# Streamed weight tiles of 1024 columns instead of 512 in a decoder block with product-key experts

## The chip, the core and the metric

The kernel runs on one core of a Trainium2 chip. The metric is the device time of one execution in microseconds (us), over the runs given below. Its matrix engine is called TensorE (PE in the profile), its elementwise engine VectorE (DVE), its activation engine ScalarE (ACT), its general engine GpSimd (POOL); SyncE (SP) issues most transfers. Sixteen DMA engines move data between memory and the on-chip buffers, and PSUM banks take what TensorE computes.

## The reference

One sequence of 1024 tokens with 1024 features goes through a mixing half and an expert half. Cut to what matters:

```python
h = rmsnorm(x, norm_mix_w)
z = h @ w_in
zs, zq, zk, zv, zg = split(z)
ya = rwkv7_time_mix(token_shift(zs, mu), ...)
yb = diff_attention(zq, zk, zv, ...)
ga, gb = split(zg)
merged = sigmoid(ga) * (ya @ proj_a) + sigmoid(gb) * (yb @ proj_b)
x = x + merged @ w_out
hf = rmsnorm(x, norm_ffn_w)
q = hf @ w_q
s = einsum('thcd,hcnd->thcn', q, sub_keys)
ids, gates = top16_of_the_pair_sums(s)       # 8 heads x 16 experts for a token
act = gelu(einsum('ced,cd->ce', u_tab[ids], hf)) * gates
x = x + einsum('ce,ced->cd', act, v_tab[ids])
return rmsnorm(x, final_norm_w)
```

`u_tab` and `v_tab` have 16384 rows (experts) of 1024 numbers.

## The kernel before

**Products in three parts.** Every large float32 product is made of three faster ones. A matrix is split into `hi`, its rounding to the faster type (ScalarE, a copy), and `lo`, the rest (VectorE, a subtraction); `hi x hi`, `hi x lo` and `lo x hi` are added up in PSUM. `wsplit` (L147) loads a streamed weight tile of 128 x 512 as `wraw`, and makes `whi` and `wlo`. `wmul` (L156) takes two such tiles for one output tile of 128 features by 512 tokens: 8 steps of 128 columns, three matmuls each. There are four buffers for `wraw` and three each for `whi` and `wlo`.

**The mixing half.** It runs for tokens 0 to 511, then for 512 to 1023 (`mix`). Each group makes 42 tiles `z` from `w_in` by `wmul`, between them four recurrent heads (`rwkv`) and four attention heads (`attention`), then the merge with `proj`, then `w_out`. A recurrent head inverts small triangles in the tile `z16`, which starts as an identity: VectorE copies the constant `eye16` into it (L370). `pick` makes queries and keeps the best 16 of each half key; `choose` makes the indices and gates of 128 tokens, in tiles `ids` and `gate`.

**The experts, for tokens 0 to 511: gathers.** `peer` (L787) does 128 tokens at a time. For each of the 128 picks, GpSimd issues a DMA that gathers one row of `u` for each token into one of five `uv` buffers (L773), and VectorE multiplies it with `hb` and sums (L795). Then the same with rows of `v`, which VectorE multiplies by `act` and adds to `acc` (L802). That makes 1024 gathers of 512 KB in all. They begin while the second group is mixed, and go on beside the rest of the kernel.

**The experts, for tokens 512 to 1023: dense.** `gates` (L804) turns the indices into a table of gates for every expert and token, `gd_s`. `dense` (L844) then goes through all experts in 128 blocks of 128. For block e, `head` makes `ua`, the product of the block of `u` and the tokens (24 matmuls, weights by `wsplit`; the first 16 blocks are made earlier, by `ahead`, and read back). ScalarE applies gelu (`gw`), VectorE multiplies it with the gates (L865) and both split it into `ah` and `al`. The block of `v` comes in two halves `vraw` of 128 x 512 (six buffers), each split into `vh` and `vl`; the left half has four pairs of buffers, the right half three. Then eight output tiles add three matmuls each. Six of them stay in PSUM banks for the whole loop (`yk`). The two others (`yr`) take a bank every second block, for two blocks at a time (`rest`), and VectorE adds that bank to `accd` (L885). `ua` and `yr` share two banks.

**What sets the order.** Tiles come from pools with a number of buffers for each name, and a new tile waits until a buffer is free. A scheduler in the build puts the instructions of every engine, and each engine's transfers, in one fixed order, from the dependencies, the buffers and its own idea of what an operation costs. On the chip each engine keeps that order, and waits where something is not there yet. So the products of the gathers stand at fixed places between the other instructions of VectorE.

Of the kernel before, what the change touches and what calls it, by code (L numbers as in the profile page):

```python
# [8 lines left out]
F32 = mybir.dt.float32  # L9
F32R = mybir.dt.float32r  # L10
BF = mybir.dt.bfloat16
I32 = mybir.dt.int32
U32 = mybir.dt.uint32
AF = mybir.ActivationFunctionType
OP = mybir.AluOpType
# [16 lines left out]
NB = 5  # L32
NW = 3
NRAW = 4
NVR = 6
# [7 lines left out]
NV = (8, 6)  # L43
# [3 lines left out]
def body(ctx: ExitStack, tc: tile.TileContext, ins, out, dbg=None):  # L47
# [49 lines left out]
    def const(name, shape, dt=F32):  # L97
        t = kp.tile(shape, dt, name=name)
        nc.sync.dma_start(t, ins[name])
        return t  # L100
# [10 lines left out]
    eye16 = const("eye16", [64, 16, 16])  # L111
    blk = const("blk", [P, P])
    rmask = const("rmask", [P, 512])
    dist = const("dist", [P, T])
    lam4 = const("lam4", [64, 4])
    eye_row = const("eye_row", [P, P])
# [30 lines left out]
    def wsplit(src):  # L147
        raw = wp.tile([P, 512], F32, name="wraw", bufs=NRAW)
        nc.sync.dma_start(raw, src)
        hi = wp.tile([P, 512], F32R, name="whi", bufs=NW)  # L150
        lo = wp.tile([P, 512], F32R, name="wlo", bufs=NW)
        nc.scalar.activation(hi, raw, AF.Copy)  # L152
        nc.vector.tensor_tensor(lo, raw, hi.bitcast(F32), op=OP.subtract)  # L153
        return hi, lo

    def wmul(o, src, xh, xl, n=8, step=1):  # L156

        w = []  # L160
        for k0 in range(0, n, step):
            ks = range(k0, k0 + step)
            for k in ks:
                if k % 4 == 0:
                    w.append(wsplit(src[k // 4]))
                hi = w[-1][0][:, (k % 4) * P:(k % 4 + 1) * P]
                nc.tensor.matmul(o, hi, xh(k), start=(k == 0), stop=False)  # L167
                nc.tensor.matmul(o, hi, xl(k), start=False, stop=False)  # L168
            for k in ks:
                lo = w[k // 4][1][:, (k % 4) * P:(k % 4 + 1) * P]  # L170
                nc.tensor.matmul(o, lo, xh(k), start=False, stop=(k == n - 1))  # L171
# [71 lines left out]
    def mix(gi, t0, W):  # L243
# [13 lines left out]
        def zt(ct):  # L257
            b = zbank("z")[:, :W]
            wmul(b, ins["w_in"][ct], lambda k: hh_[:, k, :W], lambda k: hl_[:, k, :W])
            return b  # L260
# [18 lines left out]
        def rwkv(h, kz, rz, vz):  # L279
# [90 lines left out]
            nc.vector.tensor_copy(z[nn], eye16[nn])  # L370
# [244 lines left out]
        for d in range(8):  # L615
            m = []
            for i in range(2):
                sgm = at("sgm")[:, :W]
                nc.sync.dma_start(sgm, ins["g_s"][gi, 8 * i + d, :, :W])
                b = zbank("pj")[:, :W]  # L620
                wmul(b, ins["proj"][d, i:i + 1], lambda k: yh[4 * i + k], lambda k: yl[4 * i + k], 4)
                t = mg[d // 2][:, d % 2 * 512:d % 2 * 512 + W] if i == 0 else sgm
                nc.vector.tensor_tensor(t, sgm, b, op=OP.mult)
                m.append(t)
            nc.vector.tensor_tensor(m[0], m[0], m[1], op=OP.add)
            show("mrg", m[0], (d, slice(None), slice(t0, t0 + W)))
            mcat.append(m[0])
# [11 lines left out]
        for k in range(8):  # L639
            w = [wsplit(ins["w_out"][k, i]) for i in range(2)]  # L640
            for a in range(TT):
                o = slice(a * P, (a + 1) * P)
                for i in range(2):
                    mm3(banks[2 * a + i], mh[k][:, o], ml[k][:, o], *w[i], k == 0, k == 7)
# [14 lines left out]
    def pick(t0, W, fh, fl):  # L659
# [5 lines left out]
        for hc in range(16):  # L665
# [4 lines left out]
            wmul(b, ins["wq"][hc], lambda k: fh[:, k, :W], lambda k: fl[:, k, :W])  # L670
# [134 lines left out]
    def gates(sp, a, sl, eye8):  # L805
# [24 lines left out]
    def dots(e, W, fh, fl):  # L830
        b = zbank("ua")[:, :W]
        wmul(b, ins["ut"][e], lambda k: fh[:, k, :W], lambda k: fl[:, k, :W], step=8)
        return b
# [8 lines left out]
    def dense(t0, W, fh, fl):  # L842
# [13 lines left out]
        def head(e):  # L856
# [9 lines left out]
            v = []  # L866
            ah, al = at("ah", F32R)[:, :W], at("al", F32R)[:, :W]
            split(w, ah, al)
            for h, c in enumerate(HALVES):
                raw = fp.tile([P, 512], F32, name="vraw", bufs=NVR)  # L870
                nc.sync.dma_start(raw, ins["v"][e * P:(e + 1) * P, c])
                v.append([fp.tile([P, 512], F32R, name=n, tag=f"v{h}", bufs=NV[h]) for n in ("vh", "vl")])
                split(raw, *v[h])
            return ah, al, v

        def add(o, b, r, first, last):
            ts = slice(o[0] * P, (o[0] + 1) * P)
            mm3(b, r[0][:, ts], r[1][:, ts], *r[2][o[1]], first, last)
# [40 lines left out]
    if "nopeer" not in dbg:  # L919
        with tc.tile_pool(name="sp", bufs=1) as sp:  # L920
            eye_f = sp.tile([P, P * 8], F32, name="eye_f", bufs=1)
            nc.sync.dma_start(eye_f, ins["eye8"])
            eye8 = sp.tile([P, P, 8], BF, name="eye8", bufs=1)
# [3 lines left out]
            for a, c in enumerate(late[o // P:]):  # L927
                gates(sp, a, choose(*c), eye8)
                ahead(sp, ND * P, fh, fl, range(a * NE // ND, (a + 1) * NE // ND))
# [6 lines left out]
def prepare(inputs):  # L936
# [7 lines left out]
    wt = lambda w: c(w.reshape(2, 4, P, -1, P).transpose(3, 0, 2, 1, 4).reshape(-1, 2, P, 512))  # L944
    a["w_in"] = wt(g["w_in"][0])
    a["proj"] = wt(np.concatenate([g["proj_a"][0], g["proj_b"][0]], axis=0))
    a["w_out"] = c(g["w_out"][0].reshape(8, P, 2, 512).transpose(0, 2, 1, 3))
# [3 lines left out]
    a["ut"] = c(a["u"].reshape(P, P, 2, 4, P).transpose(0, 2, 4, 3, 1).reshape(P, 2, P, 512))  # L951
# [22 lines left out]
    a["eye16"] = c(np.tile(np.eye(16, dtype=f)[None], (64, 1, 1)))  # L974
# [34 lines left out]
```

## Time and profile before

| | |
|---|---|
| runs | 3574.19 us median of 3 (3565.35 to 3584.0) |
| the profiled execution, and the span of its trace | 3566.25 us, 3564.5 us |
| busy: PE, DVE, ACT, POOL | 87%, 82%, 37%, 37% of the span |
| largest groups of DVE | products with `v` rows 655.5 us, with `u` rows 616.3 us, `wlo` 372.7 us |
| largest group of ACT | `whi` 344.4 us |
| DMA | 898.69 MB, mean 252 GB/s |

A row of a group names the line of the kernel, the engine, the operation, the tile written and the tiles read, and how often it occurs; then the time that it keeps the engine busy, and the mean of one in ns. The stretch of a timeline gives starts. Where an engine's rows overlap, as VectorE's do, since the end of one instruction lies beside the beginning of the next, what counts for the sum is the distance from one start to the next.

### The profile page before, as it was taken

How to read it: one execution, taken by the hardware profiler on the slowest of the kernel's cores; microseconds unless marked ns; L12 is line 12 of the kernel's file. 1: busy time of each engine (PE TensorE's matmuls, PEld its weight loads, DVE VectorE, ACT ScalarE, POOL GpSimd, SP SyncE). 2: the span in 40 equal slices, each digit the busy share in tenths (PEclk: the TensorE clock that was granted, in tenths of full speed). 3: DMA queues.
4: the chain of work that ended last, by engine and by line, in shares of the span. 5: the costliest groups of instructions: out<-in, count | busy, mean ns of one | idle time of the engine just before them, and what ended most of it. 6: DMA issues, size and time to landing. Idle time of an engine off the chain costs nothing. (4 is left out here: it accounts for less than half of the span.)

```text
span 3564.5 us, 50945 instructions
## 1 busy us (share of the span) xinstructions
PE 3102.8 (87%) x17382; PEld 2427.3 (68%) x17382; DVE 2929.3 (82%) x6546; ACT 1335.0 (37%) x2483; POOL 1318.3 (37%) x1036
## 2 busy tenths in 40 slices
PE   6999988998888874969888879999989999999997
PEld 5777666776666654757666657777777777777776
DVE  4555556977989897899888678999989998999997
ACT  3433523342324331223898832332222322223232
POOL 0000000014455455341122235556566555655662
PEclk9999988998989886979889989999999999999999
DMA  4222434246868778975477899999999999999995
GB/s 132 72 63 85 126 119 162 87 131 203 275 223 278 235 268 278 333 276 160 146 230 217 269 334 320 347 348 351 354 343 349 342 349 347 346 347 344 352 353 188
DMA packets 407526, 898.69 MB, mean 252 GB/s; under 512 B 69025, under 2 KB 140001, under 8 KB 403169
## 3 DMA queue, kind: packets, MB, share of 16 engines
q0 software_dynamic: 147456, 536.94, 42.9%
q1 hardware_dynamic: 259808, 358.49, 30.0%
q8 instruction: 137, 2.24, 0.3%
q14 instruction: 125, 1.02, 0.1%
HBM read 829.22 MB, written 66.07 MB: 251 GB/s over the span
## 5 line engine op out<-in xcount | busy, mean ns | idle before, releaser
L773 POOL DMA_INDIRECT uv<-u,ids x512 | 644.7, 1259 | 1210.1 <-DVE uv L795 535.9
L773 POOL DMA_INDIRECT uv<-v,ids x512 | 672.5, 1313 | 574.6 <-DVE acc L802 415.6
L802 DVE SCALAR_TENSOR_TENSOR acc<-uv,act,acc 128x1024 f32<-128x1024 f32 x512 | 655.5, 1280 | 61.2 <-DMA uv<-v,ids 54.8
L795 DVE SCALAR_TENSOR_TENSOR uv<-uv,hb 128x1024 f32<-128x1024 f32 x512 | 616.3, 1217 | 77.1 <-DMA uv<-u,ids 75.7
L152 ACT ACTIVATE whi<-wraw 128x512 fp32r<-128x512 f32 x552 | 344.4, 630 | 715.0 <-PE z L168 233.6
L167 PE MATMUL ua<-fh,whi 128*128 128x512 f32 x1024 | 424.3, 414 | 86.6 <-DVE accd L885 72.7
L153 DVE TENSOR_TENSOR wlo<-wraw,whi 128x512 fp32r<-128x512 f32 x552 | 372.7, 685 | 149.9 <-ACT whi L152 144.8
L168 PE MATMUL ua<-fl,whi 128*128 128x512 f32 x1024 | 417.2, 407 | 0.0
L178 PE MATMUL yk<-vh,ah 128*128 128x512 f32 x768 | 304.9, 397 | 23.4 <-ACT ah L174 21.9
L174 ACT ACTIVATE ah<-gw 128x512 fp32r<-128x512 f32 x128 | 80.7, 631 | 652.6 <-DVE gw L865 652.5
L179 PE MATMUL yk<-vl,ah 128*128 128x512 f32 x768 | 305.3, 398 | 5.5 <-DVE vl L175 5.5
L180 PE MATMUL yk<-vh,al 128*128 128x512 f32 x768 | 305.0, 397 | 0.3 <-DVE al L175 0.3
L167 PEld LDWEIGHTS ua<-fh,whi 128*128 128x128 f32 x1024 | 201.2, 196 | 152.9 <-DVE accd L885 94.3
L167 PE MATMUL z<-hh,whi 128*128 128x512 f32 x672 | 274.5, 409 | 0.5 <-ACT sgo L585 0.5
L171 PE MATMUL ua<-fh,wlo 128*128 128x512 f32 x1024 | 269.1, 403 | 5.9 <-DVE wlo L153 5.9
L171 PE MATMUL z<-hh,wlo 128*128 128x512 f32 x672 | 271.1, 404 | 0.0
L168 PE MATMUL z<-hl,whi 128*128 128x512 f32 x672 | 269.8, 401 | 0.0
L824 PE MATMUL gb<-oh,ohg 128*128 128x128 f32 x1024 | 226.1, 343 | 40.3 <-ACT ohg L823 38.8
L824 PEld LDWEIGHTS gb<-oh,ohg 128*128 128x128 f32 x1024 | 167.2, 211 | 102.9 <-ACT ohg L823 66.5
L168 PEld LDWEIGHTS ua<-fl,whi 128*128 128x128 f32 x1024 | 201.4, 197 | 43.1
L171 PEld LDWEIGHTS ua<-fh,wlo 128*128 128x128 f32 x1024 | 195.8, 192 | 49.4 <-DVE wlo L153 6.9
L823 ACT ACTIVATE ohg<-ohb,sl 128x128 f32<-128x128 bf16 x512 | 226.8, 526 | 2.4 <-DVE ohb L818 2.4
(320 smaller groups left out, 5708.7 us busy)
## 6 DMA issues: line engine op xcount, KB each, us to landing
wraw<-ut SPq DMA_DIRECT2D x256, 256.0 KB, 6.3
vraw<-v SPq DMA_DIRECT2D x256, 256.0 KB, 6.5
wraw<-w_in SPq DMA_DIRECT2D x168, 256.0 KB, 2.7
gd_s<-st SPq DMA_DIRECT2D x16, 2048.0 KB, 11.9
gt<-gd_s SPq DMA_DIRECT2D x32, 1024.0 KB, 9.0
wraw<-wq SPq DMA_DIRECT2D x64, 256.0 KB, 2.7
g_s<-sgo SPq DMA_DIRECT2D x32, 256.0 KB, 3.5
wraw<-proj SPq DMA_DIRECT2D x32, 256.0 KB, 3.9
```

Of the source, the lines that this page charges most:

```text
L152: nc.scalar.activation(hi, raw, AF.Copy)
L153: nc.vector.tensor_tensor(lo, raw, hi.bitcast(F32), op=OP.subtract)
L167: nc.tensor.matmul(o, hi, xh(k), start=(k == 0), stop=False)
L168: nc.tensor.matmul(o, hi, xl(k), start=False, stop=False)
L171: nc.tensor.matmul(o, lo, xh(k), start=False, stop=(k == n - 1))
L178: nc.tensor.matmul(o, ah, bh, start=first, stop=False)
L179: nc.tensor.matmul(o, ah, bl, start=False, stop=False)
L180: nc.tensor.matmul(o, al, bh, start=False, stop=last)
L773: nc.gpsimd.indirect_dma_start(out=t, out_offset=None, in_=ins[src], in_offset=bass.IndirectOffsetOnAxis(ap=ids[:, j:j + 1], axis=0))
L795: nc.vector.scalar_tensor_tensor(u, u, 1.0, hb, op0=OP.mult, op1=OP.mult, accum_out=act[:, j:j + 1])
L802: nc.vector.scalar_tensor_tensor(acc, v, act[:, j:j + 1], acc, op0=OP.mult, op1=OP.add)
L824: nc.tensor.matmul(b[:, k * P:(k + 1) * P], o3[:, k], o1[:, k], start=True, stop=True)
```

## The change

Streamed weights come in tiles of 128 x 1024: one load, one rounding and one subtraction serve all 8 steps of `wmul`, and the host lays the weights out for it. `proj` shares one tile between its two halves, and `w_out` takes its two halves from one. The buffers become two `wraw` and two each of `whi` and `wlo`. Rows of `v` come as one tile of 128 x 1024 per block, with three `vraw` and four pairs of `vh` and `vl`. Smaller edits give room back: `eye16` is no longer a constant, and GpSimd fills `z16` by two memsets; `rmask` is kept in bfloat16; `eye_row` is loaded only ahead of `gates`; `gate` and `ids` have four buffers instead of five.

```diff
-NB = 5
-NW = 3
-NRAW = 4
-NVR = 6
+NB = 4
+NW = 2
+NRAW = 2
+NVR = 3
+NV = 4
...
 CV = 2
-NV = (8, 6)
...
-    eye16 = const("eye16", [64, 16, 16])
     blk = const("blk", [P, P])
-    rmask = const("rmask", [P, 512])
     dist = const("dist", [P, T])
     lam4 = const("lam4", [64, 4])
-    eye_row = const("eye_row", [P, P])
+    rmask_f = t4("rmask_f")[:, :512]
+    nc.sync.dma_start(rmask_f, ins["rmask"])
+    rmask = kp.tile([P, 512], BF, name="rmask_b")
+    nc.vector.tensor_copy(rmask, rmask_f)
...
     def wsplit(src):
-        raw = wp.tile([P, 512], F32, name="wraw", bufs=NRAW)
+
+        raw = wp.tile([P, D], F32, name="wraw", bufs=NRAW)
         nc.sync.dma_start(raw, src)
-        hi = wp.tile([P, 512], F32R, name="whi", bufs=NW)
-        lo = wp.tile([P, 512], F32R, name="wlo", bufs=NW)
-        nc.scalar.activation(hi, raw, AF.Copy)
-        nc.vector.tensor_tensor(lo, raw, hi.bitcast(F32), op=OP.subtract)
+        hi = wp.tile([P, D], F32R, name="whi", bufs=NW)
+        lo = wp.tile([P, D], F32R, name="wlo", bufs=NW)
+        split(raw, hi, lo)
         return hi, lo
...
-    def wmul(o, src, xh, xl, n=8, step=1):
...
-        w = []
-        for k0 in range(0, n, step):
-            ks = range(k0, k0 + step)
-            for k in ks:
-                if k % 4 == 0:
-                    w.append(wsplit(src[k // 4]))
-                hi = w[-1][0][:, (k % 4) * P:(k % 4 + 1) * P]
-                nc.tensor.matmul(o, hi, xh(k), start=(k == 0), stop=False)
-                nc.tensor.matmul(o, hi, xl(k), start=False, stop=False)
-            for k in ks:
-                lo = w[k // 4][1][:, (k % 4) * P:(k % 4 + 1) * P]
-                nc.tensor.matmul(o, lo, xh(k), start=False, stop=(k == n - 1))
+    def wmul(o, w, xh, xl, ks=range(8), step=1):
...
+        hi, lo = w
+        for k0 in range(0, len(ks), step):
+            for k in ks[k0:k0 + step]:
+                c = slice(k * P, (k + 1) * P)
+                nc.tensor.matmul(o, hi[:, c], xh(k), start=(k == ks[0]), stop=False)
+                nc.tensor.matmul(o, hi[:, c], xl(k), start=False, stop=False)
+            for k in ks[k0:k0 + step]:
+                nc.tensor.matmul(o, lo[:, k * P:(k + 1) * P], xh(k), start=False, stop=(k == ks[-1]))
 
     def split(src, hi, lo):
         nc.scalar.activation(hi, src, AF.Copy)
...
             nn = slice(0, 2 * nb)
-            nc.vector.tensor_copy(z[nn], eye16[nn])
+            nc.gpsimd.memset(z[nn], 0.0)
+            nc.gpsimd.memset(z[nn].rearrange("p a b -> p (a b)")[:, 0:256:17], 1.0)
...
         for d in range(8):
             m = []
+            w = wsplit(ins["proj"][d])
             for i in range(2):
                 sgm = at("sgm")[:, :W]
                 nc.sync.dma_start(sgm, ins["g_s"][gi, 8 * i + d, :, :W])
                 b = zbank("pj")[:, :W]
-                wmul(b, ins["proj"][d, i:i + 1], lambda k: yh[4 * i + k], lambda k: yl[4 * i + k], 4)
+                wmul(b, w, lambda k: yh[k], lambda k: yl[k], range(4 * i, 4 * i + 4))
...
         for k in range(8):
-            w = [wsplit(ins["w_out"][k, i]) for i in range(2)]
+            w = wsplit(ins["w_out"][k])
             for a in range(TT):
                 o = slice(a * P, (a + 1) * P)
                 for i in range(2):
-                    mm3(banks[2 * a + i], mh[k][:, o], ml[k][:, o], *w[i], k == 0, k == 7)
...
         for a in range(TT):
...
-            v = []
             ah, al = at("ah", F32R)[:, :W], at("al", F32R)[:, :W]
             split(w, ah, al)
-            for h, c in enumerate(HALVES):
-                raw = fp.tile([P, 512], F32, name="vraw", bufs=NVR)
-                nc.sync.dma_start(raw, ins["v"][e * P:(e + 1) * P, c])
-                v.append([fp.tile([P, 512], F32R, name=n, tag=f"v{h}", bufs=NV[h]) for n in ("vh", "vl")])
-                split(raw, *v[h])
+            raw = fp.tile([P, D], F32, name="vraw", bufs=NVR)
+            nc.sync.dma_start(raw, ins["v"][e * P:(e + 1) * P, :])
+            v = [fp.tile([P, D], F32R, name=n, bufs=NV) for n in ("vh", "vl")]
+            split(raw, *v)
             return ah, al, v
...
         def add(o, b, r, first, last):
             ts = slice(o[0] * P, (o[0] + 1) * P)
-            mm3(b, r[0][:, ts], r[1][:, ts], *r[2][o[1]], first, last)
+            mm3(b, r[0][:, ts], r[1][:, ts], *(t[:, HALVES[o[1]]] for t in r[2]), first, last)
...
+            eye_row = sp.tile([P, P], F32, name="eye_row", bufs=1)
+            nc.sync.dma_start(eye_row, ins["eye_row"])
```

The other calls of `wmul` (for `w_in`, `wq` and `ut`) pass a tile of `wsplit` in the same way.

The change moves instructions. On VectorE, in the dense stage, while gathers of `v` rows go on, a piece of one cycle of two blocks stood so before (`acc<-uv,act,acc` is a gather's product, `wlo` and `vl` the subtractions, `accd` the sum that empties a `yr` bank):

```order
L802 SCALAR_TENSOR_TENSOR acc<-uv,act,acc 128x1024 x4
L153 TENSOR_TENSOR wlo<-wraw,whi 128x512
L865 TENSOR_TENSOR gw<-gw,gt 128x512
L153 TENSOR_TENSOR wlo<-wraw,whi 128x512
L802 SCALAR_TENSOR_TENSOR acc<-uv,act,acc 128x1024
L175 TENSOR_TENSOR al<-gw,ah 128x512
L175 TENSOR_TENSOR vl<-vraw,vh 128x512
L802 SCALAR_TENSOR_TENSOR acc<-uv,act,acc 128x1024 x4
L153 TENSOR_TENSOR wlo<-wraw,whi 128x512 x2
L865 TENSOR_TENSOR gw<-gw,gt 128x512
L885 TENSOR_TENSOR accd<-accd,yr 128x512
L802 SCALAR_TENSOR_TENSOR acc<-uv,act,acc 128x1024
```

In the changed kernel the piece at the same place of a cycle is:

```order
L172 TENSOR_TENSOR vl<-vraw,vh 128x1024 x2
L801 SCALAR_TENSOR_TENSOR acc<-uv,act,acc 128x1024 x4
L172 TENSOR_TENSOR wlo<-wraw,whi 128x1024
L864 TENSOR_TENSOR gw<-gw,gt 128x512
L801 SCALAR_TENSOR_TENSOR acc<-uv,act,acc 128x1024
L172 TENSOR_TENSOR al<-gw,ah 128x512
L801 SCALAR_TENSOR_TENSOR acc<-uv,act,acc 128x1024 x5
L864 TENSOR_TENSOR gw<-gw,gt 128x512
L882 TENSOR_TENSOR accd<-accd,yr 128x512
L172 TENSOR_TENSOR wlo<-wraw,whi 128x1024
```

All four halves of `vl` of a cycle are now two instructions behind the second `accd`, none is left between the products, and the products stand as four, one, five with fewer instructions between them. In other cycles of the changed kernel they stand as four and six.

On SyncE, in the same stage, the loads of one cycle were:

```order
L871 DMA vraw<-v 128x512 x3
L149 DMA wraw<-ut 128x512 x2
L871 DMA vraw<-v 128x512
L149 DMA wraw<-ut 128x512 x2
L860 DMA gt<-gd_s 128x2048
L871 DMA vraw<-v 128x512 x3
```

They are now:

```order
L868 DMA vraw<-v 128x1024 x2
L151 DMA wraw<-ut 128x1024 x2
L868 DMA vraw<-v 128x1024 x2
L151 DMA wraw<-ut 128x1024 x2
L859 DMA gt<-gd_s 128x2048
L868 DMA vraw<-v 128x1024 x2
```

The loads of `v` for two blocks now stand together, ahead of the weights for two blocks, with the table of gates (`gt`) every fourth block.

## Rows read from the trace of the kernel before

**Rows 1.** The window view by stage: busy us per engine, clock, DMA share, GB/s
```profile
core 0: us, PE busy (x) PEld busy (x) DVE busy (x) ACT busy (x) POOL busy (x), PEclk, DMA share, GB/s
700.00:1566.00 866.00, 666.22 (x4887) 513.71 (x4886) 728.30 (x1832) 275.55 (x466) 389.27 (x308) 0.84 0.74 249
1678.00:2063.00 385.00, 324.27 (x1429) 243.11 (x1427) 306.09 (x810) 323.75 (x710) 79.96 (x66) 0.89 0.69 213
2200.00:3440.00 1240.00, 1166.96 (x4903) 930.14 (x4902) 1152.95 (x1559) 356.79 (x618) 729.10 (x560) 0.98 0.96 347
3440.00:3545.00 105.00, 101.71 (x434) 80.83 (x432) 90.87 (x115) 27.98 (x48) 43.15 (x32) 1.00 0.66 238
```

**Rows 2.** TensorE's weight loads' waits, 2200 to 3440 us: total, times, longest
```profile
PEld ua L167 <- DVE accd L885: 90.8, 45, 5.1
...
PEld ua L171 <- DVE wlo L153: 0.4, 1, 0.4
```

**Rows 3.** VectorE's waits in the same stretch
```profile
DVE uv L795 <- DMA uv<-u,ids: 49.1, 60, 2.9
DVE acc L802 <- DMA uv<-v,ids: 29.0, 47, 1.9
```

**Rows 4.** Timeline of VectorE: start, us, engine, line, operation
```profile
2705.68 1.07 DVE L865 TENSOR_TENSOR gw<-gw,gt 128x512 f32<-128x512 f32 x1
2706.67 0.68 DVE L153 TENSOR_TENSOR wlo<-wraw,whi 128x512 fp32r<-128x512 f32 x1
2707.27 1.28 DVE L802 SCALAR_TENSOR_TENSOR acc<-uv,act,acc 128x1024 f32<-128x1024 f32 x1
2708.47 0.68 DVE L175 TENSOR_TENSOR al<-gw,ah 128x512 fp32r<-128x512 f32 x1
```

**Rows 5.** Timeline of VectorE in a `u` half: two products in a row
```profile
2489.31 1.22 DVE L795 SCALAR_TENSOR_TENSOR uv<-uv,hb 128x1024 f32<-128x1024 f32 x1
...
2490.45 1.22 DVE L795 SCALAR_TENSOR_TENSOR uv<-uv,hb 128x1024 f32<-128x1024 f32 x1
```

**Rows 6.** Groups of VectorE, 2200 to 3440 us: count, busy us, mean ns
```profile
L802 DVE SCALAR_TENSOR_TENSOR acc<-uv,act,acc 128x1024 f32<-128x1024 f32 x303 | 388.1, 1281 | 33.8 <-DMA uv<-v,ids 29.0
...
L795 DVE SCALAR_TENSOR_TENSOR uv<-uv,hb 128x1024 f32<-128x1024 f32 x256 | 307.0, 1219 | 49.7 <-DMA uv<-u,ids 49.1
...
L153 DVE TENSOR_TENSOR wlo<-wraw,whi 128x512 fp32r<-128x512 f32 x204 | 135.7, 686 | 0.0
...
L865 DVE TENSOR_TENSOR gw<-gw,gt 128x512 f32<-128x512 f32 x102 | 109.9, 1077 | 0.0
```

**Rows 7.** Timeline of GpSimd: two gathers issued
```profile
2706.28 1.29 POOL L773 DMA_INDIRECT uv<-v,ids  x1 [0.30 <-issue]
2708.82 1.14 POOL L773 DMA_INDIRECT uv<-v,ids  x1 [1.25 <-DVE acc L802]
```

**Rows 8.** The tile view of `uv`, 2200 to 3440 us
```profile
DMA to landing us min/median/max: 4.5/7.1/11.3
```

**Rows 9.** The page, part 3: queue, kind, packets, MB, share of 16 engines
```profile
q0 software_dynamic: 147456, 536.94, 42.9%
q1 hardware_dynamic: 259808, 358.49, 30.0%
```

**Rows 10.** Timeline of VectorE: first gate's last use, fifth gate's first write
```profile
1130.86 0.28 DVE L797 TENSOR_TENSOR act<-act,gate 128x128 f32<-128x128 f32 x1
...
1698.99 0.26 DVE L713 TENSOR_TENSOR gate<-ch 128x128 f32<-128x128 f32 x1
```

**Rows 11.** Timeline of SyncE's queue: the two constant loads
```profile
3.55 0.57 SPq L99 DMA_DIRECT2D eye<-eye  x1
...
6.26 0.58 SPq L99 DMA_DIRECT2D eye_row<-eye_row  x1
```

**Rows 12.** Line 370 in the whole span: min, median, max ns
```profile
L370 DVE COPY z<-eye x8: 277/279/383, 6.4 to 1195.3; 64x256 f32<-64x256 f32 x8
```

**Rows 13.** The tile view of `uv`, 800 to 1280 us
```profile
DMA to landing us min/median/max: 4.1/6.1/9.2
```

More of the change, by code (lines that the diff above doesn't have):

```diff
@@ L258, in zt @@
             b = zbank("z")[:, :W]
-            wmul(b, ins["w_in"][ct], lambda k: hh_[:, k, :W], lambda k: hl_[:, k, :W])
+            wmul(b, wsplit(ins["w_in"][ct]), lambda k: hh_[:, k, :W], lambda k: hl_[:, k, :W])
             return b
@@ L643, in mix @@
                 for i in range(2):
-                    mm3(banks[2 * a + i], mh[k][:, o], ml[k][:, o], *w[i], k == 0, k == 7)
+                    mm3(banks[2 * a + i], mh[k][:, o], ml[k][:, o], *(t[:, HALVES[i]] for t in w), k == 0, k == 7)
         for a in range(TT):
@@ L669, in pick @@
             b = zbank("q")[:, :W]
-            wmul(b, ins["wq"][hc], lambda k: fh[:, k, :W], lambda k: fl[:, k, :W])
+            wmul(b, wsplit(ins["wq"][hc]), lambda k: fh[:, k, :W], lambda k: fl[:, k, :W])
             q = at("pq")[:, :W]
@@ L803, in peer, with gates @@
         finish(acc, rows, pp_, "uv", NU)
-    def gates(sp, a, sl, eye8):
+    def gates(sp, a, sl, eye8, eye_row):
         e1, g = sl[:, 0:P], sl[:, 2 * P:3 * P]
@@ L831, in dots @@
         b = zbank("ua")[:, :W]
-        wmul(b, ins["ut"][e], lambda k: fh[:, k, :W], lambda k: fl[:, k, :W], step=8)
+        wmul(b, wsplit(ins["ut"][e]), lambda k: fh[:, k, :W], lambda k: fl[:, k, :W], step=8)
         return b
@@ L927, in body @@
             for a, c in enumerate(late[o // P:]):
-                gates(sp, a, choose(*c), eye8)
+                gates(sp, a, choose(*c), eye8, eye_row)
                 ahead(sp, ND * P, fh, fl, range(a * NE // ND, (a + 1) * NE // ND))
@@ L942, in prepare @@
     a["x"] = c(g["x"].reshape(T, D))
-    wt = lambda w: c(w.reshape(2, 4, P, -1, P).transpose(3, 0, 2, 1, 4).reshape(-1, 2, P, 512))
+    wt = lambda w: c(w.reshape(8, P, -1, P).transpose(2, 1, 0, 3).reshape(-1, P, D))
     a["w_in"] = wt(g["w_in"][0])
     a["proj"] = wt(np.concatenate([g["proj_a"][0], g["proj_b"][0]], axis=0))
-    a["w_out"] = c(g["w_out"][0].reshape(8, P, 2, 512).transpose(0, 2, 1, 3))
+    a["w_out"] = c(g["w_out"][0].reshape(8, P, D))
     a["wq"] = wt(g["peer_wq"][0])
@@ L950, in prepare @@
     a["u"], a["v"] = c(g["peer_u"][0]), c(g["peer_v"][0])
-    a["ut"] = c(a["u"].reshape(P, P, 2, 4, P).transpose(0, 2, 4, 3, 1).reshape(P, 2, P, 512))
+    a["ut"] = c(a["u"].reshape(P, P, 8, P).transpose(0, 3, 2, 1).reshape(P, P, D))
     a["nmw"] = c(g["norm_mix_w"][0].reshape(1, D))
@@ L973, in prepare @@
     same = (p[:, None] // CH) == (p[None, :] // CH)
-    a["eye16"] = c(np.tile(np.eye(16, dtype=f)[None], (64, 1, 1)))
     a["blk"] = same.astype(f)
```

## The prediction

> **What bounds the kernel now.** I read the table by stage first, because the shares of the whole page are averages over stages with different limits. The last long stage, the dense experts beside the gathers, is where three resources are full at once: TensorE is busy 1167 of 1240 us, VectorE 1153, and the DMA engines 96%. In the two long stages before it the DMA share is 0.74 and 0.69 [rows 1].
>
> Inside 2200 to 3440 us the waits tell which of the three sets the pace [rows 2, 3]. TensorE's weight loads for `ua` wait 90.8 us, all but a trace of it for one thing: the `accd` sum on VectorE, which has to empty a PSUM bank. VectorE waits for no other engine there; it waits 49.1 and 29.0 us for gathered rows to land. The waiting line on VectorE is therefore the pace, and the gathers feed it.
>
> That can be added up. The stretch has 102 blocks of experts (the `gw` group), so 51 cycles of two blocks, 1240 / 51 = 24.3 us each. VectorE's work in a cycle, by the distance from one start to the next: a product with a `v` row takes 1.20 us and one with a `u` row 1.14, a 512-column subtraction or `accd` sum 0.60, the `gw` product 0.98 [rows 4, 5]. With the counts of [rows 6]: (303 x 1.20 + 256 x 1.14) / 51 = 12.8; `wlo` and `vl`, 8 x 0.60 = 4.8; `gw` 2.0; `al` and `accd` 2.4. Sum 22.0, and 78.1 / 51 = 1.5 of waiting. 0.8 stays without a name; two gather blocks end in this stretch. TensorE without its 90.8 / 51 = 1.8 of waiting would need 22.5, so both lie under 24.3.
>
> **What the change does there, part by part.**
>
> *Fewer subtractions.* Two pairs of 512 columns per block become two single ones of 1024. No row shows a 1024-column subtraction. Its bounds are the two 1024-column products: 1.20, which saves nothing on 2 x 0.60, and 1.14. I take 1.14, since at 512 columns too the plain subtraction is the cheapest form in the trace. That is 0.06 to 0.07 a pair, four pairs a cycle: **-0.27 us** of VectorE work per cycle. ScalarE's rounding copies get cheaper too, and there nothing is won: ScalarE is busy 357 of 1240 us [rows 1].
>
> *The order on VectorE.* This is the larger term, and the diff doesn't show it. A gather writes into one of five `uv` buffers, so a product can start only when the gather issued after the fifth product before it has landed. From the end of a product to the next issue on GpSimd it is 0.3 us at the least: the product that starts at 2707.27 leaves VectorE some 1.28 us later, and the gather starts at 2708.82 [rows 4, 7]. Issue to landing is 7.1 us in the median, 4.5 to 11.3 [rows 8]. Together 7.4 us. I walk both listings of VectorE shown with the change with that number, time 0 at the first of the four products.
>
> Before: products 1 to 4 end at 4.8; `wlo`, `gw`, `wlo` to 6.98; product 5 to 8.18; `al` and `vl` to 9.38; products 6 to 9 run to 14.18, and each finds its buffer filled (6 needs 1.2 + 7.4 = 8.6; 9 needs 12.2); two `wlo`, `gw` and `accd` to 16.96; product 10 needs 8.18 + 7.4 = 15.6. No wait.
>
> After: products 1 to 4 end at 4.8; one `wlo` of 1.14 and `gw` to 6.92; product 5 to 8.12; `al` to 8.72. The `vl` that stood here has gone to the other one, behind `accd`. Products 6 to 9 start at 8.72, 9.92, 11.12 and 12.32, each just after its row has landed, and end at 13.52. Product 10 stands right behind them and needs 8.12 + 7.4 = 15.52: **2.0 us of wait**. Where the listing has four, then six in a row, the wait is 2.6.
>
> Counted over the whole order: of 50 cycles of the changed kernel 21 wait 2.0 and 20 wait 2.6, 9 not at all, 1.9 on average; of 48 before, 13 have a run that waits 1.4, 0.4 on average. By the walk a cycle gains 1.5 of wait and loses 0.27 of work, +1.2. The trace has 1.5 of wait per cycle where the walk has 0.4; the other 1.1 comes from landings that are later than the median. Some of these delays will fall inside the new long wait and cost nothing more. If all of them do, wait goes from 1.5 to 1.9 and the net is +0.1; if none, +1.2. I take **+0.8 per cycle**, nearer the upper end, because waits now fall on 107 of 559 products [rows 3, 6], so spread over places other than the tenth. The work beside gathers lasts 54 cycles (51, and 3 for the gathers left after 3440 us [rows 1]): **+43 us**. TensorE can't cover it: it is already waiting for `accd`, which stands behind these products.
>
> *Larger transfers.* SyncE's listing now asks for two `v` blocks and two weight tiles in one go. By the page, queue 1, which carries them, costs 30.0% for 358 MB and the gathers, in rows of 4 KB, 42.9% for 537 MB [rows 9]: 4.5% less per byte, at most 0.3 us of all DMA engines per cycle. I book nothing: the wait above is one of latency. The Trainium skill, in "Perfetto Trace Analysis", DMA Optimizations, says that going from 2 KB to 4 KB can improve throughput dramatically when the DMA is the limit. By that rule the gathers would land sooner; the two queues' cost per byte doesn't bear out "dramatically".
>
> *Deeper buffers.* `vh` and `vl` go from 4 and 3 pairs per half to 4 of both, `whi` from 1.5 tiles to 2. For `wlo` TensorE's loads wait 0.4 us in all [rows 2], and the view has no wait for `vh` or `vl`: nothing is won. `gate` and `ids` go from 5 buffers to 4, while four blocks of gathers hold one each; the first block lets its gate go at 1131 us, and the fifth is written at 1699 [rows 10]. Nothing.
>
> *The rest.* Two constant loads leave SyncE's queue ahead of `x` (0.6 us each with their gaps): -1.2 [rows 11]. `eye_row` comes back ahead of the gates, beside the eight times larger `eye8`: nothing. Eight copies of 0.28 us [rows 12] leave VectorE, and sixteen memsets take their place on GpSimd; eight of them stand between gathers, at 0.3 us of issue each [rows 7]. In the order a pair stands some 40 gathers ahead of the head that uses it, right after the head before has let the tile go, so neither the gathers behind it nor that head wait for long: bounds -2 and +3, taken as 0. The rounding of `rmask` is one copy under the first loads. In the stages before 2063 us, 164 pairs save 0.07 us each, 11 us of VectorE; TensorE or ScalarE (324 of 385 us during the gates) lead there [rows 1], so I take -2.
>
> Sum: 3566 (the profiled execution) + 43 - 3 = 3606. The median of the runs shown is 3574, 8 above that execution; on it the same +40 gives **3614 us**. A measurement of this kernel can tell about 0.5%, 18 us, from no change, so this is slower by twice that.
>
> **The rivals.**
>
> *The gathers land sooner, and it gets faster.* The wait at the tenth product is landing plus 0.3 minus 5.4; it is gone at a landing of 5.1 us. Against it: earlier, at a DMA share near 0.7, the median is still 6.1 [rows 13], and nothing in the change takes a fifth of the traffic away. For it: if the new runs make the gathers ask less densely, the queue shortens by itself, and late landings are what most of today's wait is. Then wait per cycle stays at 1.5, the work's 0.27 comes through on 54 cycles (-15), -5 elsewhere: 3554 us. The rule of the Trainium skill quoted above ("Perfetto Trace Analysis", DMA Optimizations) would bring this about through larger packets. TensorE's 22.5 us per cycle caps any further gain. Chance 0.20.
>
> *The new wait swallows the old ones.* The pause lets every late transfer catch up, net +0.1 per cycle, or the landing falls by half a microsecond: 3574 and within 18 us of it. Chance 0.22.
>
> *The bursts.* Two `v` and two `w` tiles in one go are 2.1 MB instead of 1.3; at 347 GB/s [rows 1] 0.8 MB is 2.3 us. If one more gather in each cycle lands that much later, and half of it shows, it adds 1.1 x 54 = 60 to the forecast: 3674 us. It decides if the `uv` landing rises above 8 us. Chance 0.08. The forecast itself has 0.50.
>
> That the change does nothing is excluded: the order and the sizes are in the program.
>
> **How the numbers follow.** Slower: 0.50 + 0.08 = 0.58; no difference 0.22; faster 0.20. The forecast's own range is +0.1 to +1.2 per cycle with the -3: 3577 to 3636. The range for 8 in 10 has to take in the edge of the faster case and most of the bursts: 3552 to 3662.
>
> **What would show it.** In the stretch beside the gathers, VectorE's waits for `uv` rise from 78 to about 120 us, always at the end of a run of five or six products; TensorE's wait for `accd` rises from 91 to about 130; a cycle takes 25.1 us; the DMA share falls to about 0.93; `vl` and `wlo` last 1.2 us at a count of half. It is wrong if `uv` waits stay at 78 or the landing's median falls under 6.5 (first rival), if the cycle lengthens with the landing above 8 (bursts), or if the time comes or goes before 2063 us, where I book 3.

## The result, and the profile after

The changed kernel takes **3599.20 us** (median of five runs, 3591.99 to 3611.16) against 3574.19: a ratio of **1.0077 [1.0058, 1.0097]**, so slower by 25 us. The profiled execution took 3591.99 us, its span is 3590.2. The dense stage begins no later than before: the first `yk` matmul starts at 2080.6 us, before at 2085.2. So the loss lies behind that point. By stage (answering to [rows 1]):

```profile
700.00:1566.00 866.00, 666.15 (x4864) 510.81 (x4865) 726.65 (x1767) 255.76 (x398) 405.17 (x321) 0.83 0.74 252
1678.00:2063.00 385.00, 315.38 (x1434) 234.66 (x1432) 301.27 (x791) 322.79 (x697) 72.03 (x60) 0.91 0.67 205
2200.00:3440.00 1240.00, 1152.83 (x4785) 920.24 (x4784) 1125.41 (x1340) 325.35 (x405) 756.76 (x553) 0.97 0.94 343
```

The first two stages are nearly as they were. Beside the gathers, TensorE is busy 14 us less, VectorE 27 us less, and the DMA share fell from 0.96 to 0.94: all three have more idle time. The waits in that stretch, TensorE's weight loads first, then VectorE's (answering to [rows 2, 3]):

```profile
PEld ua L165 <- DVE accd L882: 104.4, 41, 5.8
...
DVE uv L794 <- DMA uv<-u,ids: 64.8, 57, 4.0
DVE acc L801 <- DMA uv<-v,ids: 40.2, 48, 2.1
```

VectorE waits 105.0 us for gathered rows instead of 78.1, and TensorE 104.4 for VectorE's sum instead of 90.8. The granted clock of the stretch also fell, from 0.98 to 0.97. That isn't what lengthens it: VectorE sets the pace, and what it waits for TensorE's results (`gw`, by way of ScalarE) is 0.6 us in all. VectorE's groups there (answering to [rows 6]: count, then busy us and mean ns):

```profile
L801 DVE SCALAR_TENSOR_TENSOR acc<-uv,act,acc 128x1024 f32<-128x1024 f32 x298 | 382.3, 1283 | 45.7 <-DMA uv<-v,ids 40.2
L794 DVE SCALAR_TENSOR_TENSOR uv<-uv,hb 128x1024 f32<-128x1024 f32 x256 | 307.1, 1221 | 66.6 <-DMA uv<-u,ids 64.8
L172 DVE TENSOR_TENSOR wlo<-wraw,whi 128x1024 fp32r<-128x1024 f32 x100 | 121.9, 1219 | 0.0
L172 DVE TENSOR_TENSOR vl<-vraw,vh 128x1024 fp32r<-128x1024 f32 x100 | 117.6, 1217 | 0.0
L864 DVE TENSOR_TENSOR gw<-gw,gt 128x512 f32<-128x512 f32 x100 | 106.8, 1068 | 0.6 <-ACT gw L863 0.6
```

100 blocks instead of 102 went through, so a cycle of two blocks takes 1240 / 50 = 24.8 us instead of 24.3. A cycle also has more products now: 554 / 50 = 11.1 instead of 559 / 51 = 11.0. One subtraction of 1024 columns does the work of two; the timeline below has 1.13 from its start to the next (2740.52 to 2741.65). Landing of `uv` in the stretch (answering to [rows 8]), and the two queues of the page (answering to [rows 9]):

```profile
DMA to landing us min/median/max: 4.3/6.7/12.0
```

```profile
q0 software_dynamic: 147456, 536.94, 42.6%
q1 hardware_dynamic: 201552, 358.40, 29.0%
```

The median landed 0.4 us sooner, not later. What a cycle looks like now, VectorE's timeline first (start, us; in brackets the idle time before):

```profile
2731.14 0.68 DVE L882 TENSOR_TENSOR accd<-accd,yr 128x512 f32<-128x512 f32 x1
2731.74 2.35 DVE L172 TENSOR_TENSOR vl<-vraw,vh 128x1024 fp32r<-128x1024 f32 x2
2734.01 3.92 DVE L801 SCALAR_TENSOR_TENSOR acc<-uv,act,acc 128x1024 f32<-128x1024 f32 x3
2738.33 1.28 DVE L801 SCALAR_TENSOR_TENSOR acc<-uv,act,acc 128x1024 f32<-128x1024 f32 x1 [0.40 <-DMA uv<-v,ids]
2739.54 1.06 DVE L864 TENSOR_TENSOR gw<-gw,gt 128x512 f32<-128x512 f32 x1
2740.52 1.22 DVE L172 TENSOR_TENSOR wlo<-wraw,whi 128x1024 fp32r<-128x1024 f32 x1
2741.65 0.68 DVE L172 TENSOR_TENSOR al<-gw,ah 128x512 fp32r<-128x512 f32 x1
2742.26 5.24 DVE L801 SCALAR_TENSOR_TENSOR acc<-uv,act,acc 128x1024 f32<-128x1024 f32 x4
2748.37 2.61 DVE L801 SCALAR_TENSOR_TENSOR acc<-uv,act,acc 128x1024 f32<-128x1024 f32 x2 [0.88 <-DMA uv<-v,ids]
2750.90 1.07 DVE L864 TENSOR_TENSOR gw<-gw,gt 128x512 f32<-128x512 f32 x1
```

and the gathers that GpSimd issues meanwhile:

```profile
2731.49 0.94 POOL L772 DMA_INDIRECT uv<-v,ids  x1 [1.86 <-DVE acc L801]
2735.56 1.86 POOL L772 DMA_INDIRECT uv<-v,ids  x1 [3.12 <-DVE acc L801]
2737.73 1.02 POOL L772 DMA_INDIRECT uv<-v,ids  x1 [0.30 <-issue]
2739.05 1.38 POOL L772 DMA_INDIRECT uv<-v,ids  x1 [0.30 <-issue]
2740.73 1.81 POOL L772 DMA_INDIRECT uv<-v,ids  x1 [0.30 <-DVE gw L864]
```

While VectorE makes the sum and two `vl` in a row, it frees no buffer, and GpSimd stands idle for 3.12 us. Then a run of products frees one buffer every 1.2 us, and GpSimd can't follow: an issue here takes 1.02 to 1.86 us and 0.30 passes before the next. The run of six stops at its fifth product, for 0.88 us. That product needs the buffer of the one that started at 2738.33 and left VectorE at 2739.61; GpSimd was still busy with the gather before, and issued this one at 2740.73.

The loss shows in two places. The last gather is issued 7.7 us later than before, and the dense blocks that are left then take 17.7 us more. The timelines of GpSimd, VectorE (the last product) and TensorE, before:

```profile
3507.53 1.86 POOL L773 DMA_INDIRECT uv<-v,ids  x1 [1.26 <-DVE acc L802]
...
3515.74 1.28 DVE L802 SCALAR_TENSOR_TENSOR acc<-uv,act,acc 128x1024 f32<-128x1024 f32 x1
...
3543.18 0.40 PE L180 MATMUL yr<-vh,al 128*128 128x512 f32 x1
```

and after:

```profile
3515.21 1.01 POOL L772 DMA_INDIRECT uv<-v,ids  x1 [0.30 <-issue]
...
3522.72 3.92 DVE L801 SCALAR_TENSOR_TENSOR acc<-uv,act,acc 128x1024 f32<-128x1024 f32 x3
...
3568.52 0.39 PE L177 MATMUL yr<-vh,al 128*128 128x512 f32 x1
```

By the fixed order, 980 products stood ahead of the 118th block's `gw` before, and 988 do now. So when the gathers end, fewer blocks are done: behind the last product there are still four `gw` instead of two.

### The profile page after: what moved, and what is told of

Its sections match the earlier page's. It is cut to its first block, busy times and chain, and to the rows that moved or that the text cites. A ratio compares the mean times of both kernels' runs of the same rounds, so it can differ in the third digit from the quotient of the medians.

```text
span 3590.2 us, 48734 instructions
## 1 busy us (share of the span) xinstructions
PE 3102.6 (86%) x17382; PEld 2429.1 (68%) x17382; DVE 2902.7 (81%) x6135; ACT 1270.0 (35%) x2075; POOL 1368.3 (38%) x1052
## 3 DMA queue, kind: packets, MB, share of 16 engines
q0 software_dynamic: 147456, 536.94, 42.6%
## 4 chain that ended last, share of the span: by engine, by line
PE 30%; DVE 20%; issue 18%; DMA 17%; POOL 8%; ACT 7%; SPq 0%; POOLq 0%; DVEq 0%; ACTq 0%
POOL uv L772 8%; DMA uv<-v,ids 7%; DMA uv<-u,ids 5%; ACT ohg L822 4%; DVE uv L794 3%; PE z L165 3%; PE z L168 3%; PE z L166 3%; DVE acc L801 3%; DVE wlo L172 2%; DVE gw L864 2%; PE sc L525 1%; ACT st L824 1%; PE ua L165 1%; DVE vl L172 1%
## 5 line engine op out<-in xcount | busy, mean ns | idle before, releaser
L772 POOL DMA_INDIRECT uv<-u,ids x512 | 684.3, 1337 | 1101.7 <-DVE uv L794 449.2
L171 ACT ACTIVATE whi<-wraw 128x1024 fp32r<-128x1024 f32 x276 | 292.1, 1060 | 761.7 <-issue 214.7
L165 PE MATMUL ua<-fh,whi 128*128 128x512 f32 x1024 | 435.1, 425 | 104.3 <-DVE accd L882 89.5
L172 DVE TENSOR_TENSOR wlo<-wraw,whi 128x1024 fp32r<-128x1024 f32 x276 | 336.4, 1219 | 128.0 <-ACT whi L171 127.7
L166 PE MATMUL ua<-fl,whi 128*128 128x512 f32 x1024 | 427.9, 418 | 0.0
```

The source lines that it names most:

```text
L165: nc.tensor.matmul(o, hi[:, c], xh(k), start=(k == ks[0]), stop=False)
L166: nc.tensor.matmul(o, hi[:, c], xl(k), start=False, stop=False)
L171: nc.scalar.activation(hi, src, AF.Copy)
L172: nc.vector.tensor_tensor(lo, src, hi.bitcast(F32), op=OP.subtract)
L772: nc.gpsimd.indirect_dma_start(out=t, out_offset=None, in_=ins[src], in_offset=bass.IndirectOffsetOnAxis(ap=ids[:, j:j + 1], axis=0))
```

## The experiments

**Theory 1**: the change put the products of the gathers in longer runs on VectorE, and the ring of five buffers can't feed such a run. **Rivals**: the size of the transfers; the tiles or buffers of 1024 columns by themselves; the throughput of the DMA engines; TensorE's sum standing behind longer runs.

For all of them, one count from each trace. It takes the products of gathers 460 to 999, sorts them by their place in a run (a run ends at a `gw`, `wlo`, `vl` or `accd`), and adds up VectorE's gaps of over 0.12 us ahead of them. Rows that follow without a gap overlap by some 0.075 us, and a gap is counted from there. The last column is the time from the end of the last product to the end of the span. All are us, but for the count.

| kernel | median us | those 540 products took | fifth or later in a run | wait ahead of these | wait ahead of the others | after the last product |
|---|---|---|---|---|---|---|
| before | 3574 | 1197.5 | 6 | 4.8 | 81.6 | 47.5 |
| changed | 3599 | 1209.8 | 92 | 42.6 | 72.4 | 63.6 |
| transfers split | 3602 | 1216.9 | 92 | 49.3 | 73.0 | 62.9 |
| `v` in halves | 3598 | 1228.0 | 56 | 37.1 | 86.7 | 52.1 |
| only `v` wide | 3611 | 1217.1 | 77 | 35.1 | 81.6 | 62.4 |
| work in halves | 3591 | 1228.4 | 87 | 66.8 | 44.2 | 44.4 |
| small edits | 3578 | 1203.9 | 6 | 3.9 | 91.0 | 46.8 |
| small edits, six buffers | 3494 | 1140.5 | 6 | 4.6 | 20.1 | 47.2 |
| small edits, seven buffers | 3491 | 1126.3 | 6 | 3.0 | 7.9 | 47.7 |
| changed, made room | 3600 | 1212.6 | 92 | 42.5 | 75.6 | 63.8 |
| changed, six buffers | 3534 | 1157.4 | 92 | 27.4 | 31.6 | 64.7 |
| `v` in halves, six buffers | 3534 | 1164.5 | 58 | 23.2 | 18.3 | 52.8 |
| changed, one `vraw` | 3701 | 1284.1 | 73 | 31.0 | 93.5 | 78.6 |
| changed, one `vraw`, six buffers | 3665 | 1257.2 | 73 | 8.6 | 41.5 | 81.5 |

### The size of the transfers

The changed kernel, each tile filled by two transfers of 512 columns:

```diff
-        nc.sync.dma_start(raw, src)
+        for c in HALVES:
+            nc.sync.dma_start(raw[:, c], src[:, c])
...
-            nc.sync.dma_start(raw, ins["v"][e * P:(e + 1) * P, :])
+            for c in HALVES:
+                nc.sync.dma_start(raw[:, c], ins["v"][e * P:(e + 1) * P, c])
```

> The changed kernel, but each 1024-column tile of weights and of v is filled by two transfers of 512 columns, as before; rounding and subtraction stay at 1024. VectorE keeps the changed order (runs of five or six products of the gathers). Theory (the order bunches the products, and the fifth or sixth waits for its gather's landing): as slow as the changed kernel, 3590 to 3610 us, waits of VectorE for uv in 2200 to 3440 us 105 to 125 us. Rival (larger transfers in bursts delay the gathers): like the kernel before, 3570 to 3582 us, waits near 80 us.

Measured: 3601.63 us, ratio 1.0082 [1.0061, 1.0102]. VectorE's waits for `uv` in the stretch are 111.6 us, inside the expected 105 to 125. The transfers are back at 256 KB, and the packets near the number of before (page, parts 3 and 6):

```profile
q1 hardware_dynamic: 259728, 358.43, 29.3%
...
wraw<-ut SPq DMA_DIRECT2D x256, 256.0 KB, 6.2
vraw<-v SPq DMA_DIRECT2D x256, 256.0 KB, 6.2
```

So the larger transfers neither cost nor give anything that can be measured. The Trainium skill ("Perfetto Trace Analysis", DMA Optimizations) says that batching transfers from 2 KB to 4 KB can improve throughput dramatically where the DMA is the limit. Here the queue's share is 29.0% with the larger and 29.3% with the smaller ones. As a sixth buffer shows below, the DMA engines were not the limit, so no run here tests the rule where it is meant to hold.

### One half of the change at a time

The changed kernel with the loads, tiles and split of `v` in halves as before (weights stay wide); the numbers of buffers go with them:

```diff
-NVR = 3
-NV = 4
+NVR = 6
+NV = (8, 6)
```

> The changed kernel with the rows of v in halves of 512 again (load, rounding, subtraction and buffers as before); weights stay at 1024. In its order a vl stands again between most runs of products; walked with 7.4 us from release to landing a cycle waits 0.9 us (0.6 before, 2.0 in the changed kernel). Theory: the loss is gone but for a small rest, 3568 to 3582 us. Rival (large weight transfers or 1024-column instructions as such): at least half of the loss stays, 3586 us or more.

Measured: 3597.53 us, 1.0071 [1.0050, 1.0093]. A miss: nearly the whole loss stays. The walk missed too: it gave this order 0.9 us of wait per cycle and the changed one 2.0, and in the table this kernel waits 123.8 us in all and the changed one 115.0. The kernel before with only `v` wide (the lines of `head` and `add` from the change, and the same buffers):

```diff
-NVR = 6
+NVR = 3
...
-NV = (8, 6)
+NV = 4
```

> The kernel before with only the rows of v at 1024 columns (and their buffers as in the change); weights at 512. Walked as above a cycle waits 1.6 us. Theory: most of the loss is there, 3585 to 3605 us. Rival (the weights' part of the change is to blame): 3570 to 3580 us.

Measured: 3611.24 us, 1.0100 [1.0079, 1.0120]: `v` alone costs at least as much. (Its profiled execution reached the dense stage 19 us later than that of the kernel before, 2104.0 against 2085.2; from there to the end it took 35 us more, the changed kernel 30.) The halves don't add up. The count gives a reason why they needn't: each alone already makes the runs longer (56 and 77 products in fifth place or later, from 6), and each waits 35 to 37 us there.

### Large loads and tiles, work in halves

```diff
-        split(raw, hi, lo)
+        for c in HALVES:
+            split(raw[:, c], hi[:, c], lo[:, c])
...
-            split(raw, *v)
+            for c in HALVES:
+                split(raw[:, c], *(t[:, c] for t in v))
```

> The changed kernel with its large loads, tiles and buffers, but each tile is rounded and subtracted in two halves of 512. VectorE's order still has runs of five and six products (both blocks' vl stand together behind accd); the walk gives 1.7 us of wait per cycle. Theory: the loss stays, 3588 to 3608 us, though no instruction is longer than before. Rival (the 1024-column instructions delay what stands behind them): 3565 to 3580 us.

Measured: 3590.52 us, 1.0042 [1.0024, 1.0061]. The time falls in the expected range, and 17 of the 25 us stay though every subtraction has 512 columns again. The order is still one with long runs (87 products), and VectorE waits 111.0 us in all. So the length of the instructions isn't what costs most.

### The small edits, and a sixth buffer

The kernel before with the small edits alone, which give the room for a sixth `uv` buffer, and then with that:

```diff
-NU = 5
+NU = 6
```

> The kernel before with only the small edits of the change (identity built by two fills, rounded mask kept in 16 bits, one constant row loaded late, four id and gate buffers). Every theory: no difference that can be measured, 3565 to 3585 us, since the orders on VectorE and of the gathers in the dense stage are those of before; uv waits of VectorE between 2220 and 3480 us near 89 us. It is the base for the run with six gather buffers.

> The small edits and six gather buffers in place of five; 512-column tiles, order on VectorE as in the kernel before. Theory 1 (the ring of five buffers with some 7 us from release to landing sets the rate of gathers): 3520 to 3550 us; VectorE's uv waits between 2220 and 3480 us fall from 89 to under 45 us; issue-to-landing stays under 8 us. Rival (the DMA engines' throughput sets the rate): 3565 to 3580 us, and issue-to-landing grows from 7.1 to about 9 us, since one more gather waits in the queue.

Measured: 3577.95 us, 1.0010 [0.9990, 1.0029], and **3494.43 us, 0.9777 [0.9751, 0.9803]**. The small edits are free. The sixth buffer gives 84 us, more than expected; VectorE's waits and the landing in the same stretch (two views):

```profile
DVE uv L797 <- DMA uv<-u,ids: 19.9, 30, 2.1
DVE acc L804 <- DMA uv<-v,ids: 1.9, 3, 1.2
...
DMA to landing us min/median/max: 4.9/7.4/11.9
```

21.8 us of waits are left from 78.1, while the landing rose by 0.3 only. The throughput of the DMA engines was not the limit; the five buffers were. Part of the gain lies earlier, where gathers run beside the mixing of the second group: in the profiled execution the first `yk` matmul starts at 2068.4 us, 17 us sooner than before.

The changed kernel had no room for a sixth. One wide tile and one raw buffer fewer make it, and were run alone first:

```diff
-NR2 = 4
+NR2 = 3
...
-NVR = 3
+NVR = 2
```

> The changed kernel with three instead of four wide tiles in the mixing stages and two instead of three raw buffers for v, which frees the room for a sixth gather buffer that the next run uses; five gather buffers still. Theory 1 and rivals: 3590 to 3612 us, as the changed kernel; if the raw buffers of v matter, above 3612.

> The run before with six gather buffers; order on VectorE as in the changed kernel. Theory 1 (the longer runs of products cost only because five buffers can't feed them): the loss of the change goes, within 10 us of the 512-column kernel with six buffers, 3520 to 3555 us, uv waits of VectorE under 50 us in place of 118. Rival A (the sum from PSUM now stands behind longer runs of products, so TensorE waits whatever the buffers): it stays 20 to 30 us above the 512-column kernel with six buffers, and TensorE's accd wait stays at 90 us or more. Rival B (DMA throughput): 3590 to 3612 us, no gain.

Measured: 3599.58 us, 1.0076 [1.0046, 1.0106], and 3533.81 us, 0.9882 [0.9858, 0.9907]. The sixth buffer gives 66 us here too, but the distance to the 512-column kernel is 39 us, not under 10. The time lies in theory 1's range of 3520 to 3555 only because the 512-column kernel came out faster than expected. Theory 1 in its simple form falls: five buffers are not the reason that the change costs time, as the same change costs no less with six. Rival A, which said 20 to 30 above, is nearer in time, but its other condition, 90 us of waiting in TensorE, is not met:

```profile
PEld ua L165 <- DVE accd L882: 66.5, 32, 4.1
...
DVE uv L794 <- DMA uv<-u,ids: 41.4, 39, 3.1
DVE acc L801 <- DMA uv<-v,ids: 12.2, 21, 1.3
```

VectorE still waits 53.6 us for rows, 31.8 more than the 512-column kernel with six; by the table, 22.8 of a difference of 34.3 lie ahead of the fifth and later products. With five buffers the difference was 28.6. So a sixth buffer lowers the waits of both kernels and leaves the distance between them. The other part lies behind the gathers: in the last column the wide kernel takes 17.5 us more, with five buffers 16.1. Two blocks more are left there. Their work on VectorE is about 4.4 us each (an estimate from the distances 1.13, 0.98 and 0.60), so that some 9 us are only moved behind the gathers, and the rest is lost there.

The traces show what is late in a long run. In the changed kernel with five buffers (means over those of the 540 gathers that have a landing), a gather that takes the buffer of the first product of a run is issued 0.5 us after the product ends and lands 7.0 us later; for the second to fifth it is 1.0 to 1.3 and 6.7 to 7.1, for a sixth 1.1 and 8.4 (28 gathers).

### Taking the pair of subtractions apart

One raw buffer for `v` in the changed kernel, then the same with the sixth `uv` buffer:

```diff
-NVR = 3
+NVR = 1
```

> The changed kernel with one raw buffer for v instead of three. The tiles and the operations stay; on VectorE the two 1024-column vl of a cycle come apart, one of them now stands between the runs of products (four products, vl, gw, al, wlo, five products), where the changed kernel has both behind the second accd. Theory 1 (the places of the products between the other work set the wait): most of the loss goes, 3572 to 3588 us, uv waits of VectorE between 2220 and 3480 us under 100 us instead of 118. Rival A (the loss has nothing to do with the places; any tile of 1024 columns costs it): 3592 to 3612 us. Rival C (a single raw buffer is late): above 3612 us, and VectorE or ScalarE waits for vraw.

> The run before with six gather buffers (and three wide tiles in the mixing stages for the room). Theory 1: 3490 to 3512 us, level with the 512-column kernel with six buffers (3494), since the places of the products are nearly as favourable. Rival A: 3525 to 3545 us, as the changed kernel with six buffers (3534). Rival C: above that, with waits for vraw.

Measured: 3700.58 us, 1.0319 [1.0298, 1.0340], and 3664.54 us, 1.0218 [1.0202, 1.0233]. Rival C. The waits with six buffers, VectorE's and then ScalarE's:

```profile
DVE vl L172 <- ACT vh L171: 74.6, 31, 5.7
DVE uv L794 <- DMA uv<-u,ids: 38.7, 38, 2.4
DVE acc L801 <- DMA uv<-v,ids: 6.0, 8, 1.7
...
ACT vh L171 <- DMA vraw<-v: 377.6, 52, 13.5
```

`vl` waits for ScalarE, which waits for the one raw tile: a new wait of about 75 us in the stretch. The runs didn't come apart as expected either, with 73 products in fifth place or later. Their waits are 31.0 us with five buffers and 8.6 with six, but VectorE stands still for `vl` as well, which gives the gathers time. These two runs decide nothing on the order.

### A seventh buffer, and the weights' half with six

The kernel with the small edits and six buffers gets a seventh:

```diff
-NR2 = 4
+NR2 = 3
...
-NU = 6
+NU = 7
...
-NVR = 6
+NVR = 5
```

> The 512-column kernel with six gather buffers gets a seventh (three wide tiles in the mixing stages and five raw half tiles of v for the room; order on VectorE in the dense stage unchanged). Theory 1 (latency through the ring): the 25 us of uv waits that are left nearly go and TensorE's accd wait falls under 30 us: 3470 to 3488 us. Rival B (at a DMA share of 97% the throughput is the limit now): 3488 to 3502 us, and issue to landing grows from 7.6 us towards 9.5.

Measured: 3491.12 us, 0.9747 [0.9723, 0.9770]; the kernel before took 3588.56 beside it, so the ratio is what compares. It can't be told from the six buffers. Nor does it decide between the two expectations: 3491 us lies in rival B's range, and 0.9747 of the usual 3574, 3484 us, in theory 1's; the waits of the 540 products fell from 24.7 to 10.9 us, and the trace has no landings. The window view of the stretch says why little is left to win:

```profile
2200.00:3440.00 1240.00, 1220.00 (x5211) 979.54 (x5210) 1221.13 (x1648) 383.72 (x658) 777.98 (x585) 1.00 0.98 365
```

TensorE and VectorE are now both busy over 98% of it. The kernel with six or seven buffers and 512 columns is the version that beats both of the comparison.

Last, the run with wide weights and `v` in halves gets a sixth buffer:

```diff
-NR2 = 4
+NR2 = 3
...
-NU = 5
+NU = 6
...
-NVR = 6
+NVR = 4
```

> The run with weights in 1024 columns and rows of v in halves (3598 us with five gather buffers, where runs of five products are as frequent as in the changed kernel) gets a sixth gather buffer (three wide tiles in the mixing stages and four raw half tiles of v for the room; order on VectorE in the dense stage unchanged). Theory 1 (the weights' part of the change costs only through the fifth product of a run and the ring of five): its whole loss goes, 3488 to 3504 us, level with the 512-column kernel with six buffers (3494), and waits of the fifth and later products of a run fall from 37 to under 12 us. Rival A (tiles of 1024 columns of weights cost something that the ring has nothing to do with): it keeps some 20 us over that kernel, 3510 to 3530 us.

Measured: 3533.61 us, 0.9882 [0.9860, 0.9903]. It misses theory 1's range, and lies just above rival A's. The waits of the fifth and later products fell from 37.1 to 23.2, not under 12, with nearly the same number of such products. VectorE has a new wait as well, of `vl` for ScalarE, which the smaller number of raw tiles may have brought; that wasn't separated:

```profile
DVE vl L172 <- ACT vh L171: 9.9, 11, 2.1
```

**What stands.** The loss is independent of the size of the transfers and of the small edits. Every kernel of the table with 1024-column tiles has long runs and, the two with one raw buffer aside, some 35 to 67 us of waiting at their end with five buffers, 23 to 27 with six, against 3 to 5 in the 512-column kernels. A second part is the order too, but not a wait: with `v` at 1024 columns and worked on whole, fewer blocks are done when the gathers end, and 62 to 65 us follow the last product instead of 47, with five buffers as with six (79 to 82 with one raw buffer). The converse, 1024-column tiles in an order with short runs, couldn't be tried cleanly: the order follows from the buffers, and the one setting meant to change it starved `vl`. So the order as the cause is argued from the traces, not shown by a run of its own.

## Why the prediction was right, and where it was off

**Direction and place hold.** Slower by 25 us, all in the dense stage; the term named as the larger one, longer runs on VectorE against a ring of gather buffers, is where the traces put the new waits. That the runs are the cause is argued, as said above, and that it takes a ring of only five is refuted: with six the change costs 39 us.

**The size of that term was too large.** Forecast +0.8 us per cycle, 54 cycles, +43; measured 24.8 against 24.3, +0.5, some 27. It lies between the two ends given, +0.1 and +1.2. The wait per cycle rose from 1.5 to 105.0 / 50 = 2.1, by 0.6, not by the 1.1 that +0.8 and the saving of 0.27 imply. The step that was mis-sized is how much of the walk's new wait coincides with the old ones. The prediction let 0.4 of its 1.5 us go that way; it was 0.9. And it is not the old delays that went, as "some of these delays will fall inside the new long wait" has it: the waits ahead of products one to four fell from 81.6 to 72.4 only, 0.2 us per cycle. The new wait itself came out at half, 37.8 us more in the 49 cycles of the count, 0.8 per cycle instead of 1.5.

**The walk had three faults.** It took one latency from release to landing, 7.4 us, for all places; the trace has 7.5 for the first product of a run and 9.5 for the sixth. It set the wait "always at the end of a run of five or six": in the trace the fourth product alone waits 51.3 of 115.0 us, and landings scatter from 4.3 to 12.0. And it put the run with `v` in halves at less than half of the changed kernel's wait, where the two are level. The mechanism is borne out by the traces in kind; its price was taken from too smooth a picture.

**Part luck.** The waits and the subtractions give +0.6 - 0.27, and more products in a cycle, 11.1 instead of 11.0, another 0.1, which the prediction didn't have. That the sum over 54 cycles, 27, lies so near the 25 measured is no proof of the sum: from the first `yk` matmul to the last product the changed kernel takes 14.2 us more (1446.0 against 1431.8), behind the last product 16.1 more, and it had started 4.6 sooner.

**Subtractions.** Taken 1.14 from start to start; the timeline has 1.13. The saving of 0.27 per cycle was there and was outweighed. The Trainium skill ("Perfetto Trace Analysis", Optimizing Scalar/DVE Operations) says that grouping into larger operations can improve throughput if the engine is saturated. The trace agrees as to the work: VectorE was busy 93% of the stretch, and 1.13 us replace 2 x 0.60. The waits grew by more.

**TensorE's wait for `accd`**: forecast about 130, measured 104.4. `uv` waits: about 120, measured 105.0. Cycle: 25.1, measured 24.8. DMA share: 0.93, measured 0.94.

**Booked at nothing or at 3 us, and too small to measure**: larger transfers (the split run is level with the changed kernel), the small edits (1.0010), the stages before 2063 us.

**The rivals.** "The gathers land sooner": the median did come down, 7.1 to 6.7, but the waits rose. "The bursts" would need the landing above 8 us: no. "The new wait swallows the old ones" is true for 9 us of the 540 products' waits, and no more; with the landing down by 0.4, the loss is still clear of noise.

**Not named.** The order also puts 8 more products ahead of the 118th block, so the dense blocks run on for 53 us after the last gather is issued instead of 36. The prediction counted cycles beside the gathers and left this split out. It shifts where the 25 us appear, and by the estimate above nearly half of the 16 us behind the last product is not a shift but a cost.

## What to carry to other kernels

When a change coarsens the tiles of an engine that works through a fixed order, look at what else stands in that order: here 0.27 us of work per cycle were saved and 0.6 us of waiting came in, most of it at the end of the longer runs of products that depend on gathers. If such products wait for landings, hold the time from release to landing against the number of buffers times the consumer's pace, and spend on-chip memory on that ring first: one more buffer of 4 KB per partition took 2.2% off, almost three times what the change lost. It did not make up for the order: with six buffers the wide tiles cost 39 us.

## What was not expected

- A sixth gather buffer is worth 84 us (3577.95 to 3494.43), though the DMA engines were already at a share of 0.96; it went to 0.97, and landing rose by 0.3 us only.
- The two halves of the change cost 24 and 38 us alone (against 3573.7 beside them) and 25 together.
- GpSimd's issue of a gather takes 1.4 us on average over the 540 of the changed kernel (mostly 0.9 to 2.0), and 0.3 more to the next, longer than the 1.2 us product that frees the buffer. Where VectorE stands idle during it (14 of them), it takes 0.94. Within a run the gathers fall behind: with six buffers and `v` in halves, the issue after a run's first product starts 0.6 us after it, after the fifth 2.0, and the landing takes 7.3 and 8.3 us.
